# Seven block products for three column groups instead of two, and weight sums added by DMA

## The chip, the cores and the metric

The kernel runs on one core of a Trainium2 chip. Time is device time in microseconds (us) of one execution, the median of several runs. Lower is better.

## The reference, cut to what matters

A decoder trunk of four layers on 256 tokens of width 1024. In each layer a token mixer and a memory attention share one input and one output projection, and a SwiGLU feed-forward follows:

```python
SEQ, D_MODEL, D_FF = 256, 1024, 2816

def _swiglu(x, w_in, w_out):              # w_in: 1024 x 5632, w_out: 2816 x 1024
    gu = x @ w_in
    return (jax.nn.silu(gu[..., :D_FF]) * gu[..., D_FF:]) @ w_out

# for each of the four layers
x = x + jnp.concatenate([mix, mo], axis=-1) @ w_o[i]
x = x + _swiglu(_rmsnorm(x, g_ffn[i]), w_ffn_in[i], w_ffn_out[i])
```

All is float32. The change touches the first feed-forward product (`x @ w_in`) and the part of the second that is computed by the same helper.

## The kernel before, in words

**How a product is made.** Every float32 operand is split into a high and a low part (`wparts`, L128 to L133): ScalarE (ACT) casts the raw weight tile to `whi` (L131), VectorE (DVE) subtracts to get `wlo` (L132). One product of 128 tokens, 128 rows of the weight and 512 columns is then three matmuls (L136 to L138): high by high, high by low, low by high. A weight tile `raw` is 128 partitions by 2 by 512 floats, 512 KB; it is loaded by a DMA that SyncE issues (L124, and L220 in the helper below). The pool of raw tiles has eight buffers, and so have `whi` and `wlo`. A load waits until the tile that had its buffer before has been read for the last time.

**The first feed-forward product** runs over six column groups b = 0 to 5 of w_in: for b = 0 to 4, 512 columns of the gate half and 512 of the up half; for b = 5, 256 of each. A plain group (`proj`, twice) makes 2 token halves x 8 row tiles x 2 sides x 3 = 96 matmuls of 512 columns from 8 raw tiles.

**The helper `strassen`** (L197 to L260) computes the same group as a 2 by 2 block product by seven block products instead of eight: 7 x 12 = 84 matmuls. Its left blocks are sums of token blocks (`ab`), its right blocks are sums of weight blocks. Of the weight blocks b11, b12, b22, b21 (two raw tiles each, s = 0, 1) eight tile sums are needed: t = b11 + b12, b12 += b22, t += b22, t += b21, for each s. In the kernel before all eight are VectorE additions of 128x1024 floats (`plus`, L224). Each right block is then split by `wparts`, so the helper splits 14 tiles, against 8 of a plain group. The tile t (`wsum`) lives in the same pool of eight raw buffers. The matmuls of the helper are L214 to L216; its partial results go through `v`, `u`, `y` (VectorE, 128x512) and the callback `out`.

It is used for b = 1 and b = 4, and once per layer in the second feed-forward product (`hidden_products`, on eight of its 22 row blocks): three times per layer, 12 times in all. For the last use, `hidden_side` builds the token sums from the transposed hidden blocks of b = 3 and b = 4.

**What sets the order.** The engines run side by side, each through its own list, and wait for each other on semaphores. The lists come from a scheduler that reorders within the program's dependences: loads on SyncE's queue, casts on ACT, subtractions and sums on DVE. Small callbacks (`later`, `flush`) put transposes and evacuations between the matmuls. GpSimd (POOL) has little to do: it computes the norms' reciprocal roots (`rstd`, L329 and L330) and a few masks.

Of the kernel before, what the change touches and what calls it, by code (L numbers as in the profile page):

```python
# [13 lines left out]
ALU = mybir.AluOpType  # L14
# [3 lines left out]
P = 128  # L18
# [22 lines left out]
def trunk_kernel(ctx, tc, x, mem, vecs, w_in, w_kv, w_o, w_f1, w_f2, lams, g_final, out):  # L41
    nc = tc.nc
# [85 lines left out]
    def wparts(raw, nk=2, ncol=512):  # L128
        hi = wsplit.tile([P, nk, ncol], F32R, name="whi", tag="whi")
        lo = wsplit.tile([P, nk, ncol], F32R, name="wlo", tag="wlo")  # L130
        nc.scalar.copy(hi, raw)  # L131
        wlast[:] = [nc.vector.tensor_tensor(lo, raw, hi.bitcast(F32), ALU.subtract)]  # L132
        return hi, lo  # L133
# [9 lines left out]
    def later(rounds, f):  # L143
        pend.append([rounds, f])

    def flush():
        for item in pend:
            item[0] -= 1
        for item in [i for i in pend if i[0] <= 0]:
            pend.remove(item)  # L150
            item[1]()
# [45 lines left out]
    def strassen(left, right, ab, out):  # L197

        acc = {}
        banks = {1: 1, 2: 1, 5: 5, 3: 5, 7: 7, 4: 7, 6: 6}

        def product(p, w, s):
            b = banks[p]
            if b not in acc:
                acc[b] = ps_acc.tile([P, 512], F32, name="acc", tag="ps")
            lh, ll = ab[p]  # L210
            for k in range(2):
                kc = 2 * s + k
                start, stop = kc == 0 and p == b, kc == 3
                nc.tensor.matmul(acc[b], lh[:, kc, :], w[0][:, k, :], start=start, stop=False, skip_group_check=True)  # L214
                nc.tensor.matmul(acc[b], lh[:, kc, :], w[1][:, k, :], start=False, stop=False, skip_group_check=True)  # L215
                nc.tensor.matmul(acc[b], ll[:, kc, :], w[0][:, k, :], start=False, stop=stop, skip_group_check=True)  # L216

        def load(cols, r):
            raw = wraw.tile([P, 2, 512], F32, name="raw", tag="raw")
            nc.sync.dma_start(raw, cols[r:r + 2 * P, :].rearrange("(c p) n -> p c n", p=P))  # L220
            return raw

        def plus(out, a, b):
            nc.vector.tensor_tensor(out, a, b, ALU.add)  # L224

        part = lambda name: work.tile([P, 512], F32, name=name, tag="att", bufs=NATT)
        b22, sums = [], []
        v, u, y = part("sv"), part("su"), part("sy")
        for s in range(2):
            b11, b12 = (load(c, 2 * s * P) for c in (left, right))  # L230
            b22.append(load(right, 512 + 2 * s * P))
            product(1, wparts(b11), s)
            t = wraw.tile([P, 2, 512], F32, name="wsum", tag="raw")
            plus(t, b11, b12)
            if s == 1:
                nc.scalar.copy(v, acc[1])
            product(5, wparts(t), s)
            flush()
            plus(b12, b12, b22[s])
            product(7, wparts(b12), s)  # L240
            plus(t, t, b22[s])
            product(6, wparts(t), s)
            flush()
            sums.append(t)
        plus(u, acc[6], v)
        plus(y, acc[7], u)
        b21 = [load(left, 512 + 2 * s * P) for s in range(2)]
        for s in range(2):
            product(2, wparts(b21[s]), s)
        out(0, 0, acc[1], None)  # L250
        out(1, 1, acc[5], y)
        flush()
        for s in range(2):
            plus(sums[s], sums[s], b21[s])
            product(4, wparts(sums[s]), s)
            if s == 1:
                out(1, 0, acc[7], u)
            product(3, wparts(b22[s]), s)
            flush()
        out(0, 1, acc[5], u)  # L260

    def negative(rs):
        out = []
# [443 lines left out]
    for i in range(DEPTH):  # L707
# [136 lines left out]
        hab, hsum = {}, {}  # L844

        def hidden_side(k, t, src):

            tt, stt = nc.vector.tensor_tensor, nc.vector.scalar_tensor_tensor
            if k == 0 and t == 0:
                both = big.tile([P, 2, 4, P], F32, name="hsum", tag="big")  # L850
                hsum["d"], hsum["a21"] = both[:, 0], both[:, 1]
                nc.scalar.copy(hsum["d"], src)
            elif k == 0:
                nc.scalar.copy(hsum["a21"], src)
                tt(hsum["d"], hsum["d"], src, ALU.subtract)
                hab[7] = token_parts(hsum["d"])
            elif t == 1:
                tt(hsum["a21"], src, hsum["a21"], ALU.subtract)
                hab[5] = token_parts(hsum["a21"])
                stt(hsum["d"], hsum["d"], -1.0, src, ALU.mult, ALU.subtract)  # L860
                hab[6] = token_parts(hsum["d"])
            else:
                stt(hsum["a21"], src, -1.0, hsum["d"], ALU.mult, ALU.subtract)
                hab[3] = token_parts(hsum["a21"])
                for p, g, t in ((1, 3, 0), (2, 4, 0), (4, 4, 1)):
                    hab[p] = tuple(x[:, :, t * P:(t + 1) * P] for x in hts[g])

        for b in range(6):
            n = 512 if b < 5 else 256
            if n == 512:  # L870
                hh = big.tile([P, 4, S], F32R, name="hh", tag="big")
                hl = big.tile([P, 4, S], F32R, name="hl", tag="big")
            else:
                both = big.tile([P, 2, 2, S], F32R, name="hb", tag="big")
                hh, hl = both[:, 0], both[:, 1]
            hts.append((hh, hl))
            sg = [work.tile([P, 512], F32, name="sg", tag="qkn", bufs=4) for _ in range(NT)]

            def h_out(t, g_ps, u_ps, hh=hh, hl=hl, sg=sg, n=n, b=b):
                s = sg[t][:, :n]  # L880
                if g_ps is not None:
                    nc.scalar.activation(s, g_ps, AF.Silu, scale=rx[t])
                if u_ps is not None:
                    nc.vector.scalar_tensor_tensor(s, u_ps, rx[t], s, ALU.mult, ALU.mult)
                    later(1, lambda: hidden(t, s, hh, hl, n, b))

            def hidden(t, s, hh, hl, n, b):
                tr = ps_x.tile([P, 4, P], F32, name="tr", tag="ps")
                for c in range(n // P):
                    nc.tensor.transpose(tr[:, c, :], s[:, c * P:(c + 1) * P], ident)  # L890
                src = tr[:, :n // P, :]
                hi = hh[:, :, t * P:(t + 1) * P]
                nc.scalar.copy(hi, src)
                nc.vector.tensor_tensor(hl[:, :, t * P:(t + 1) * P], src, hi.bitcast(F32), ALU.subtract)
                if b in (3, 4):
                    hidden_side(b - 3, t, src)

            c0 = b * 512
            gcols, ucols = w_f1[i, :, c0:c0 + n], w_f1[i, :, DFF + c0:DFF + c0 + n]
            if b in (1, 4):  # L900
                def gated(t, side, ps, add, sg=sg, hh=hh, hl=hl, b=b, up={}):
                    if side == 0:
                        src = ps
                        if add is not None:
                            nc.vector.tensor_tensor(sg[t], ps, add, ALU.add)
                            src = sg[t]
                        nc.scalar.activation(sg[t], src, AF.Silu, scale=rx[t])
                        up[t, 0] = sg[t]
                    else:
                        up[t, 1] = add if t == 1 else work.tile([P, 512], F32, name="sx", tag="att", bufs=NATT)  # L910
                        nc.vector.tensor_tensor(up[t, 1], ps, add, ALU.add)  # L911
                    if (t, 0) in up and (t, 1) in up:
                        nc.vector.scalar_tensor_tensor(sg[t], up[t, 1], rneg[t], sg[t], ALU.mult, ALU.mult)
                        later(2, lambda: hidden(t, sg[t], hh, hl, 512, b))

                strassen(gcols, ucols, ab, gated)
            elif n == 512:
                proj([gcols], xT, lambda t, ps: h_out(t, ps, None))
                if b == 0:
                    ab, rneg = tokens_side(xg, xT), negative(rx)  # L920
                proj([ucols], xT, lambda t, ps: h_out(t, None, ps))
            else:
                proj([gcols, ucols], xT, lambda t, ps: h_out(t, ps[:, :n], ps[:, n:2 * n]))
# [52 lines left out]
```

## Time and profile before

| | |
|---|---|
| median of 3 runs | 1271.62 us (1271.61 to 1271.62) |
| profiled execution, its own time | 1271.41 us |
| span of its instructions | 1269.7 us, so 1.7 us lie around it |
| PE (matmul) busy | 1258.3 us, 99% |
| DVE busy | 1022.4 us, 81% |
| ACT busy | 753.3 us, 59% |
| POOL busy | 55.7 us, 4% |
| DMA engines, mean busy share | 55.6% for 226.31 MB of loads and stores |
| granted TensorE clock | 0.999 |

The page divides the span into 40 slices and gives for each the busy tenths of every engine and of the 16 DMA engines. The matmul rows overlap each other (a matmul is shown for 0.39 us, the next starts before it has ended), so that a rate is read from the starts and not from the durations.

### The profile page before, as it was taken

The numbers are of one execution on the slowest core, as the hardware profiler recorded it, in microseconds if no ns is written. First come the engines' busy times: TensorE is split into PE (matmuls) and PEld (weight loads), VectorE is DVE, ScalarE is ACT, GpSimd is POOL, SyncE is SP. The second block draws the span as 40 slices with busy tenths as digits, with TensorE's granted clock in tenths as the row PEclk, the third lists the DMA queues.
The fourth block names the chain that finished last, engine by engine and source line by source line (L and its number), as shares of the span: only waits on it lengthen the run. The fifth ranks groups of instructions, "written<-read, shape, count | busy, mean of one in ns | idle before, by whom it ended". The sixth has DMA issues, their size and how long they took to land.

```text
span 1269.7 us, 16380 instructions
## 1 busy us (share of the span) xinstructions
PE 1258.3 (99%) x6031; PEld 1036.9 (82%) x6031; DVE 1022.4 (81%) x1271; ACT 753.3 (59%) x1067; POOL 55.7 (4%) x109
## 2 busy tenths in 40 slices
PE   8999999999999999999999999999999999999997
PEld 6888888888888888888888888888888888888886
DVE  6765699899867669989986777989996646997995
ACT  7756466575555646656655545656556655674743
POOL 1000000000111000000000000000000001000001
PEclk9999999999999999999999999999999999999999
DMA  9644538366764444836575563665486444384561
GB/s 345 203 150 133 149 116 276 106 207 193 261 193 130 136 149 116 282 116 219 192 247 172 164 197 103 185 215 180 166 272 209 133 133 149 100 260 138 199 200 66
DMA packets 111888, 227.35 MB, mean 179 GB/s; under 512 B 7488, under 2 KB 20288, under 8 KB 111808
## 3 DMA queue, kind: packets, MB, share of 16 engines
q1 hardware_dynamic: 111808, 226.31, 55.6%
q8 instruction: 47, 0.77, 0.2%
q14 instruction: 33, 0.27, 0.1%
HBM read 225.23 MB, written 1.05 MB: 178 GB/s over the span
## 4 chain that ended last, share of the span: by engine, by line
PE 95%; DVE 2%; ACT 1%; issue 1%; DMA 0%; SPq 0%; POOL 0%; POOLq 0%; ACTq 0%
PE acc L136 23%; PE acc L138 23%; PE acc L137 23%; PE acc L214 6%; PE acc L216 6%; PE acc L215 6%; PE tr L890 2%; PE tr L363 1%; DVE wlo L132 1%; PE tr L349 1%; PE tr L432 1%; PE at L413 1%; PE at L445 1%; PE at L479 1%; PE at L521 1%; DVE wsum L224 1%
## 5 line engine op out<-in xcount | busy, mean ns | idle before, releaser
L132 DVE TENSOR_TENSOR wlo<-raw,whi 128x1024 fp32r<-128x1024 f32 (+1 forms) x428 | 508.0, 1210 | 101.3 <-ACT whi L131 99.0
L131 ACT CAST whi<-raw 128x1024 fp32r<-128x1024 f32 (+1 forms) x428 | 434.1, 1041 | 198.8 <-PE acc L138 122.6
L136 PE MATMUL acc<-whi,xth 128*128 128x512 f32 (+1 forms) x896 | 353.6, 395 | 1.1 <-ACT xth L356 1.1
L137 PE MATMUL acc<-wlo,xth 128*128 128x512 f32 (+1 forms) x896 | 342.9, 383 | 1.3 <-DVE wlo L132 1.3
L138 PE MATMUL acc<-whi,xtl 128*128 128x512 f32 (+1 forms) x896 | 343.9, 384 | 0.0
L138 PEld LDWEIGHTS acc<-whi,xtl 128*128 128x128 f32 x896 | 168.4, 188 | 33.8
L137 PEld LDWEIGHTS acc<-wlo,xth 128*128 128x128 f32 x896 | 168.9, 189 | 32.3 <-DVE wlo L132 2.5
L136 PEld LDWEIGHTS acc<-whi,xth 128*128 128x128 f32 x896 | 168.7, 188 | 32.5 <-ACT xth L356 1.6
L131 ACT CAST whi<-wsum 128x1024 fp32r<-128x1024 f32 x72 | 75.7, 1052 | 85.4 <-DVE wsum L224 81.5
L132 DVE TENSOR_TENSOR wlo<-wsum,whi 128x1024 fp32r<-128x1024 f32 x72 | 87.7, 1218 | 1.5 <-ACT whi L131 0.7
L214 PE MATMUL acc<-whi,sh 128*128 128x512 f32 x192 | 75.9, 396 | 0.0
L136 PE MATMUL acc<-whi,hh 128*128 128x512 f32 x192 | 75.6, 394 | 0.0
L216 PE MATMUL acc<-whi,sl 128*128 128x512 f32 x192 | 74.9, 390 | 0.0
L138 PE MATMUL acc<-whi,hl 128*128 128x512 f32 x192 | 74.8, 390 | 0.0
L215 PE MATMUL acc<-wlo,sh 128*128 128x512 f32 x192 | 74.8, 390 | 0.0
L137 PE MATMUL acc<-wlo,hh 128*128 128x512 f32 x192 | 74.8, 390 | 0.0
L224 DVE TENSOR_TENSOR wsum<-wsum,raw 128x1024 f32<-128x1024 f32 x48 | 57.8, 1218 | 0.3
L136 PE MATMUL acc<-whi,oh 128*128 128x512 f32 x128 | 51.1, 400 | 0.0
L138 PE MATMUL acc<-whi,ol 128*128 128x512 f32 x128 | 50.0, 391 | 0.0
L137 PE MATMUL acc<-wlo,oh 128*128 128x512 f32 x128 | 49.9, 390 | 0.0
L214 PEld LDWEIGHTS acc<-whi,sh 128*128 128x128 f32 x192 | 36.1, 188 | 8.2 <-DVE sy L911 1.1
L216 PEld LDWEIGHTS acc<-whi,sl 128*128 128x128 f32 x192 | 36.1, 188 | 7.7
(236 smaller groups left out, 1762.9 us busy)
## 6 DMA issues: line engine op xcount, KB each, us to landing
raw<-in_w_ffn_in SPq DMA_DIRECT2D x160, 512.0 KB, 4.5
raw<-in_w_in SPq DMA_DIRECT2D x100, 512.0 KB, 4.8
raw<-in_w_ffn_out SPq DMA_DIRECT2D x88, 512.0 KB, 4.4
raw<-in_w_o SPq DMA_DIRECT2D x40, 512.0 KB, 4.1
raw<-in_w_mem_kv SPq DMA_DIRECT2D x16, 512.0 KB, 4.4
raw<-in_w_ffn_in SPq DMA_DIRECT2D x32, 256.0 KB, 3.2
raw<-in_w_in SPq DMA_DIRECT2D x8, 256.0 KB, 5.6
x<-in_x SPq DMA_DIRECT2D x4, 256.0 KB, 3.9
```

Of the source, the lines that this page charges most:

```text
L131: nc.scalar.copy(hi, raw)
L132: wlast[:] = [nc.vector.tensor_tensor(lo, raw, hi.bitcast(F32), ALU.subtract)]
L136: nc.tensor.matmul(ps, lh, wh, start=first, stop=False)
L137: nc.tensor.matmul(ps, lh, wl, start=False, stop=False)
L138: return nc.tensor.matmul(ps, ll, wh, start=False, stop=last)
L214: nc.tensor.matmul(acc[b], lh[:, kc, :], w[0][:, k, :], start=start, stop=False, skip_group_check=True)
L215: nc.tensor.matmul(acc[b], lh[:, kc, :], w[1][:, k, :], start=False, stop=False, skip_group_check=True)
L216: nc.tensor.matmul(acc[b], ll[:, kc, :], w[0][:, k, :], start=False, stop=stop, skip_group_check=True)
L224: nc.vector.tensor_tensor(out, a, b, ALU.add)
L349: last_pe = nc.tensor.transpose(ps[:, c, :], src[:, kc * P:(kc + 1) * P], ident).ins
L363: nc.tensor.transpose(ps[:, c, :], src[:, c * P:(c + 1) * P], ident)
L890: nc.tensor.transpose(tr[:, c, :], s[:, c * P:(c + 1) * P], ident)
```

## The change

Three things are changed.

1. The helper is used for b = 2 as well: four uses per layer instead of three, two of them next to each other (b = 1, b = 2).
2. Of the eight tile sums of a use, two (t = b11 + b12) stay on VectorE. The other six are DMAs that GpSimd issues, from a raw tile in SBUF into another one with `accum_op=add` (`add_by_dma`, L227 and L228 of the changed kernel).
3. The order of the products within the helper is different, so are the places of the two loads of b21: products 1, 5, 1, 5, then 7, 7, the loads of b21, then 6, 6, 2, 2, 3, 3, 4, 4 (before: 1, 5, 7, 6 for each s, 2, 2, then 4, 3, 4, 3). The results come out with (0, 1) before (1, 0), and `hidden_side` follows that: it keeps the transposed block of token half 0 in PSUM until that of half 1 has come.

```diff
+        def add_by_dma(out, a):
+            nc.gpsimd.dma_start(out, a, accum_op=ALU.add)
+
+        b12, b22, sums = [], [], []
         v, u, y = part("sv"), part("su"), part("sy")
         for s in range(2):
-            b11, b12 = (load(c, 2 * s * P) for c in (left, right))
+            b11 = load(left, 2 * s * P)
+            b12.append(load(right, 2 * s * P))
             b22.append(load(right, 512 + 2 * s * P))
             product(1, wparts(b11), s)
             t = wraw.tile([P, 2, 512], F32, name="wsum", tag="raw")
-            plus(t, b11, b12)
+            plus(t, b11, b12[s])
+            add_by_dma(b12[s], b22[s])
             if s == 1:
                 nc.scalar.copy(v, acc[1])
             product(5, wparts(t), s)
-            flush()
-            plus(b12, b12, b22[s])
-            product(7, wparts(b12), s)
-            plus(t, t, b22[s])
-            product(6, wparts(t), s)
+            add_by_dma(t, b22[s])
             flush()
             sums.append(t)
+        for s in range(2):
+            product(7, wparts(b12[s]), s)
+        b21 = [load(left, 512 + 2 * s * P) for s in range(2)]
+        flush()
+        for s in range(2):
+            product(6, wparts(sums[s]), s)
+            add_by_dma(sums[s], b21[s])
         plus(u, acc[6], v)
         plus(y, acc[7], u)
-        b21 = [load(left, 512 + 2 * s * P) for s in range(2)]
         for s in range(2):
             product(2, wparts(b21[s]), s)
         out(0, 0, acc[1], None)
         out(1, 1, acc[5], y)
         flush()
         for s in range(2):
-            plus(sums[s], sums[s], b21[s])
+            product(3, wparts(b22[s]), s)
+        out(0, 1, acc[5], u)
+        flush()
+        for s in range(2):
             product(4, wparts(sums[s]), s)
-            if s == 1:
-                out(1, 0, acc[7], u)
-            product(3, wparts(b22[s]), s)
-            flush()
-        out(0, 1, acc[5], u)
+        out(1, 0, acc[7], u)
...
-            elif t == 1:
+            elif t == 0:
+                hsum["a12"] = src
+            else:
...
-            else:
-                stt(hsum["a21"], src, -1.0, hsum["d"], ALU.mult, ALU.subtract)
+                stt(hsum["a21"], hsum["a12"], -1.0, hsum["d"], ALU.mult, ALU.subtract)
...
-            if b in (1, 4):
+            if b in (1, 2, 4):
```

How the lists of the engines move, at two places. First VectorE's list in the second feed-forward product of the second layer, where the helper's use begins. The numbers name single tiles: before, raw_5619, 5621 and 5623 are b11, b12 and b22 of s = 0, and wsum_5636 is its t.

```order
L132 TENSOR_TENSOR wlo_5626<-raw_5619,whi_5625 128x1024
L224 TENSOR_TENSOR wsum_5636<-raw_5619,raw_5621 128x1024
L224 TENSOR_TENSOR raw_5621<-raw_5621,raw_5623 128x1024
L132 TENSOR_TENSOR wlo_5639<-wsum_5636,whi_5638 128x1024
L132 TENSOR_TENSOR wlo_5651<-raw_5621,whi_5650 128x1024
L224 TENSOR_TENSOR wsum_5636<-wsum_5636,raw_5623 128x1024
L224 TENSOR_TENSOR wsum_5689<-raw_5673,raw_5675 128x1024
L132 TENSOR_TENSOR wlo_5663<-wsum_5636,whi_5662 128x1024
```

The same place in the changed kernel: 5683, 5685 and 5687 are b11, b12 and b22 of s = 0, 5715 and 5717 are b11 and b12 of s = 1, and wsum_5700 and wsum_5731 are the two t.

```order
L132 TENSOR_TENSOR wlo_5704<-wsum_5700,whi_5703 128x1024
L132 TENSOR_TENSOR wlo_5722<-raw_5715,whi_5721 128x1024
L224 TENSOR_TENSOR wsum_5731<-raw_5715,raw_5717 128x1024
L132 TENSOR_TENSOR wlo_5736<-wsum_5731,whi_5735 128x1024
L132 TENSOR_TENSOR wlo_5747<-raw_5685,whi_5746 128x1024
L132 TENSOR_TENSOR wlo_5758<-raw_5717,whi_5757 128x1024
L132 TENSOR_TENSOR wlo_5772<-wsum_5700,whi_5771 128x1024
L132 TENSOR_TENSOR wlo_5784<-wsum_5731,whi_5783 128x1024
```

The in-place sums (`raw<-raw`, `wsum<-wsum,raw`) are gone from VectorE, and splits of tiles that a DMA has added to (raw_5685, raw_5717, then the two wsum) follow each other directly.

Second, GpSimd's list in the feed-forward of the second layer. Before, only the four instructions of the feed-forward norm stand there, and behind them comes the next layer's norm:

```order
L329 TENSOR_SCALAR rstd_4384<-ss_4382 128x1
L330 TENSOR_TENSOR rstd_4384<-rstd_4384,nhalf_99 128x1
L329 TENSOR_SCALAR rstd_4436<-ss_4434 128x1
L330 TENSOR_TENSOR rstd_4436<-rstd_4436,nhalf_99 128x1
L329 TENSOR_SCALAR rstd_5935<-ss_5933 128x1
```

In the changed kernel 24 DMAs stand there as well. These are the norm, the six DMAs of b = 1 and the first two of b = 2 (for each use b12 += b22 and t += b22 for s = 0 and 1, then twice t += b21; in b = 1 raw_4676 and raw_4715 are b12, raw_4678 and raw_4717 b22, raw_4765 and raw_4767 b21):

```order
L228 DMA raw_4676<-raw_4678 128x1024
L335 TENSOR_SCALAR rstd_4416<-ss_4414 128x1
L336 TENSOR_TENSOR rstd_4416<-rstd_4416,nhalf_99 128x1
L335 TENSOR_SCALAR rstd_4468<-ss_4466 128x1
L336 TENSOR_TENSOR rstd_4468<-rstd_4468,nhalf_99 128x1
L228 DMA raw_4715<-raw_4717 128x1024
L228 DMA wsum_4691<-raw_4678 128x1024
L228 DMA wsum_4729<-raw_4717 128x1024
L228 DMA wsum_4691<-raw_4765 128x1024
L228 DMA wsum_4729<-raw_4767 128x1024
L228 DMA raw_4871<-raw_4873 128x1024
L228 DMA wsum_4886<-raw_4873 128x1024
```

One DMA stands ahead of the feed-forward norm, 23 behind it. Each of them waits on GpSimd's queue for its two tiles, and those behind it wait with it.

More of the change, by code (lines that the diff above doesn't have):

```diff
@@ L226, in strassen @@
         part = lambda name: work.tile([P, 512], F32, name=name, tag="att", bufs=NATT)
-        b22, sums = [], []
+        def add_by_dma(out, a):
+            nc.gpsimd.dma_start(out, a, accum_op=ALU.add)
+        b12, b22, sums = [], [], []
         v, u, y = part("sv"), part("su"), part("sy")
         for s in range(2):
-            b11, b12 = (load(c, 2 * s * P) for c in (left, right))
+            b11 = load(left, 2 * s * P)
+            b12.append(load(right, 2 * s * P))
             b22.append(load(right, 512 + 2 * s * P))
```

## The prediction

> **What bounds the kernel now.** I first read the page's head and the stalls of TensorE.
>
> ```profile
> span 1269.7 us, 16380 instructions
> PE 1258.3 (99%) x6031; PEld 1036.9 (82%) x6031; DVE 1022.4 (81%) x1271; ACT 753.3 (59%) x1067; POOL 55.7 (4%) x109
> PE 95%; DVE 2%; ACT 1%; issue 1%; DMA 0%; SPq 0%; POOL 0%; POOLq 0%; ACTq 0%
> PE acc L137 <- DVE wlo L132: 1.3, 3, 0.8
> ```
>
> TensorE is the path: 95% of the chain, and the longest of its waits for another engine is 1.3 us in total. So matmuls that go away are time that goes away, as long as the other engines keep up. What a matmul is worth has to be read from starts, since the rows overlap. Two rows of a plain group, with 36 matmuls from the first to the second:
>
> ```profile
> 170.08 0.39 PE L136 MATMUL acc<-whi,xth 128*128 128x512 f32 x1
> 178.24 0.39 PE L136 MATMUL acc<-whi,xth 128*128 128x512 f32 x1
> ```
>
> That is (178.24 - 170.08) / 36 = 0.2267 us, not the 0.39 us of a row. A plain group of 96 takes 21.8 us of TensorE, a group by seven products (84) takes 19.0 us.
>
> The view by stages shows who else is near the limit. The second line is the group b = 1 by seven products, the third the plain b = 2, the last one a whole feed-forward of the second layer:
>
> ```profile
> core 0: us, PE busy (x) PEld busy (x) DVE busy (x) ACT busy (x) POOL busy (x), PEclk, DMA share, GB/s
> 184.20:204.00 19.80, 19.80 (x90) 16.01 (x89) 19.77 (x22) 13.57 (x16) 0.00 (x0) 1.00 0.62 193
> 204.00:226.00 22.00, 22.00 (x104) 18.07 (x103) 18.60 (x19) 12.78 (x16) 0.00 (x0) 1.00 0.81 277
> 470.00:646.00 176.00, 176.00 (x803) 144.81 (x802) 164.21 (x179) 109.05 (x130) 1.49 (x4) 1.00 0.58 185
> ```
>
> In a group by seven products VectorE has no gap at all (19.77 of 19.80 us), and in the whole feed-forward it works 93%. The DMA engines work 58% there. So TensorE is first and VectorE is just behind it; the change takes work from both and gives work to the DMA engines.
>
> How far the splits run ahead of TensorE decides what a late split costs. VectorE's first split for b = 1 and TensorE's first matmul of it:
>
> ```profile
> 173.77 1.22 DVE L132 TENSOR_TENSOR wlo<-raw,whi 128x1024 fp32r<-128x1024 f32 x1
> 184.17 0.39 PE L214 MATMUL acc<-whi,xth 128*128 128x512 f32 x1
> ```
>
> The lead is 184.17 - 173.77 = 10.4 us, and more it cannot be: eight split buffers of six matmuls last 8 x 6 x 0.2267 = 10.9 us.
>
> **The change part by part.**
>
> *The third group, on TensorE.* 12 matmuls fewer per layer, 48 in all: 48 x 0.2267 = -10.9 us. All of it is on the path. This is the whole gain there can be.
>
> *VectorE and ACT.* These rows carry it:
>
> ```profile
> L224 DVE TENSOR_TENSOR wsum<-wsum,raw x48: 1208/1218/1227, 177.8 to 1232.7; 128x1024 f32<-128x1024 f32 x48
> L224 DVE TENSOR_TENSOR wsum<-raw x24: 1217/1223/1483, 151.7 to 1217.2; 128x1024 f32<-128x1024 f32 x24
> L224 DVE TENSOR_TENSOR raw<-raw x24: 1210/1224/1227, 153.4 to 1221.9; 128x1024 f32<-128x1024 f32 x24
> 307.06 1.22 DVE L132 TENSOR_TENSOR wlo<-wsum,whi 128x1024 fp32r<-128x1024 f32 x1
> 308.19 0.68 DVE L936 TENSOR_TENSOR x<-x,acc 128x512 f32<-128x512 f32 x1
> ```
>
> 96 sums become 32. One takes 1.22 us in its row, but the next instruction starts 1.13 us after it (308.19 - 307.06). VectorE loses 64 x 1.13 = 72 us, and gains 6 more splits in each of the four new uses, 24 x 1.13 = 27 us, beside their partial results (`u`, `y` and the callbacks). ACT gains 24 casts of 1.05 us at 59% load. None of it is on the path, so I cost it at nothing; TensorE's 99% covers it. In one use VectorE has 14 splits and two sums left, 16 x 1.13 = 18.1 us beside its partial results, against 22 x 1.13 = 24.9 us before. The `tr` block that is now kept in PSUM holds one of eight banks a little longer; I cost it at nothing for the same reason.
>
> *The accumulating DMAs.* There are 6 x 16 = 96. The trace shows none. Two prices matter, the time each takes of the 16 DMA engines, S, and the time until it has landed. For S the nearest rows are those of the loads:
>
> ```profile
> PE   8999999999999999999999999999999999999997
> DMA  9644538366764444836575563665486444384561
> GB/s 345 203 150 133 149 116 276 106 207 193 261 193 130 136 149 116 282 116 219 192 247 172 164 197 103 185 215 180 166 272 209 133 133 149 100 260 138 199 200 66
> L220 SPq DMA_DIRECT2D raw<-in_w_ffn_in x64: 367/368/689, 142.1 to 1164.4; - x64
> DMA to landing us min/median/max: 3.5/4.0/6.4
> ```
>
> In the first slice the engines are full at 345 GB/s, so that a 512 KB load takes 524,288 / 345,000 = 1.52 us of them. An accumulating DMA writes as many bytes as a load, so I put the lower bound at S = 1.52. It reads two operands, its source and its destination; if the two reads simply add, S = 3.04. I take the middle, 2.28: two streams are read, but from SBUF and not from HBM. For the landing, a load needs at best 3.5 us, 1.98 more than its 1.52; with SyncE's 0.37 us to issue, an accumulating DMA lands 0.37 + 2.28 + 1.98 = 4.6 us after its turn, and 2.28 later, 6.9 us, where a load shares the engines with it. I take the mean, 5.8 us. The VectorE sum that it replaces took 1.13 us, so each tile comes 4.6 us later.
>
> The Trainium skill prices such a DMA too. In "Collectives: The Full Stack", section "The bandwidth ceiling: the fold count and why AG ≠ RS ≠ AR", it says of an adding DMA that it "isn't slower because the CCE add costs cycles — it's slower because the add needs two source reads", at half the rate. No row here shows it. By it S is 3.04, which is the second rival below.
>
> Now the DMA engines' sum for one use of the helper: eight loads, 8 x 1.52 = 12.2 us, and six accumulating DMAs, 6 x 2.28 = 13.7 us, together 25.8 us, while TensorE wants the group in 19.0 us. They fall behind by 6.8 us per use. Over the whole feed-forward they do not: 0.58 x 176 = 102 us now, with 24 x 2.28 = 55 us more 157 of 173 us. So what counts is the lead at the start of a use. It is 10.4 us behind a plain group, and the later landing takes 4.6 of it, which leaves 5.8 us. Two uses in a row (b = 1, b = 2) fall behind by 13.6 us, 7.8 more than that; the single ones (b = 4 and the second product) by 6.8, 1.0 more. That is 7.8 + 1.0 + 1.0 = 9.8 us of waiting per layer, 39 us in four layers.
>
> What stands behind such a wait: on POOL the next DMAs of the use, in order, and at one place the norm's `rstd`, whose result VectorE waits for already.
>
> ```profile
> DVE rneg L266 <- POOL rstd L330: 8.0, 8, 1.5
> SPq L124 <- DVE wlo L132: 653.5, 274, 12.5
> SPq L220 <- DVE wlo L132: 279.7, 87, 15.3
> ```
>
> On SyncE's queue the loads stand behind a buffer that is not free: 87 loads of the helper already wait 279.7 us for a split to be done. A tile that is split later is freed later, and the next group's loads with it. On VectorE the splits that follow each other in the list wait for the one whose tile has not landed.
>
> *The sum.* 1271.4 (the profiled execution's own time) - 10.9 + 39 = 1299.5 us. The runs' median is 0.2 us above that execution, so I say 1300.
>
> **The rivals.**
>
> *First: the DMAs are hidden, the kernel is faster.* With S = 1.52 a use needs 12.2 + 9.1 = 21.3 us, falls behind by 2.2, two in a row by 4.5; the landing is then 0.37 + 1.52 + 1.98 to 1.52 more, on the mean 4.6 us, 3.5 later than the sum. The lead left is 6.9 us, more than 4.5. Then nothing waits and the time is 1271.6 - 10.9 = 1260.7 us; the last us may go to VectorE, which still has some 24 us per use with its partial results. For it: the DMA engines have 42% of the feed-forward free, and SBUF reads may overlap each other. Against it: two operands through an engine at the price of one.
>
> *Second: the two reads add, much slower.* S = 3.04: a use needs 30.4 us, 11.4 too many. The landing is 5.4 to 8.4, on the mean 6.9 us, 5.8 later, which leaves 4.6 us of lead. Per layer (22.8 - 4.6) + 2 x (11.4 - 4.6) = 31.8 us of waiting, 127 in all: 1271.6 - 10.9 + 127 = 1388 us. For it: the plain count of bytes read. Against it: the reads are not from HBM, which may be what limits a load.
>
> *Third: no change.* Waiting and gain are equal where the two uses in a row lose 2.7 us per layer. With lead 10.4 - (0.37 + 1.5 S + 1.98 - 1.13) = 9.2 - 1.5 S and a lag of 2 x (12.2 + 6 S - 19.0), that is at S = 1.90. This is also the point from which the change decides against itself: above 1.90 us of DMA time per sum it is slower, below it is faster. A narrow case, some 0.05 us of S on either side.
>
> A price of issue enters too: SyncE's 0.37 us is a hardware queue's row, POOL's is not shown. In "DMA: Bandwidth & Descriptors", section "Specifications", the Trainium skill gives a first byte after about 1 us for DMAs from GpSimd and 0.6 for those of SyncE; by an estimate from that, each landing is 0.4 us later, and the sum 0.4 x 3 x 4 = 5 us higher. No row here shows it.
>
> **How the numbers follow.** A difference of 0.2% is about what a measurement of this kernel can tell from none. I give my forecast (S between about 1.95 and 2.7) a chance of 0.47; the hidden DMAs 0.25; the added reads, or anything slower than S = 2.7, 0.20; no change 0.08. So faster 0.25, same 0.08, slower 0.67. The likeliest case's own range is 1275 to 1350. The range reaches down to the first rival's 1260.7 and a little below, and up to 1380, which takes in the cheaper part of the second: 1259 to 1380.
>
> **What would show each step right or wrong.** TensorE should have 48 matmuls fewer, and its starts still be 0.2267 us apart where it runs. In the list of DMA issues the accumulating ones should land some 5 to 7 us after their issue; at 4 us the first rival is right, at 8 and more the second. In the table by stages the DMA share of the two groups in a row should be over 0.9, and the waits of TensorE should name `wlo` or `whi` of the helper's splits, those of ACT the accumulating DMAs. VectorE should show gaps in these groups where it now has none. My forecast is wrong if TensorE's idle time stays near its present 11 us, and my reason is wrong if the idle time is there while the DMA engines are not full: then it is the landing or the queue on POOL, and not the engines' time.

## The result and the profile after

The changed kernel takes 1328.52 us (median of 4 runs, 1327.49 to 1330.04), the kernel before 1271.61 us: a ratio of 1.0448 with a 95% interval of 1.0433 to 1.0464. It is 56.9 us slower. The forecast was slower by 28 us, with the time measured inside its range: the direction was right, the size was half of what came.

The head of the page, the row of the granted clock in 40 slices (in tenths of full speed) and the row of GpSimd's DMA queue (packets, MB, share of 16 engines), after the change:

```profile
span 1327.4 us, 16744 instructions
PE 1270.3 (96%) x5983; PEld 1039.7 (78%) x5983; DVE 989.3 (75%) x1251; ACT 778.9 (59%) x1095; POOL 139.0 (10%) x205
PEclk9999999999999999899999999998999999989999
...
q0 software_dynamic: 13824, 50.34, 20.4%
```

The clock's row of the kernel before, for comparison:

```profile
PEclk9999999999999999999999999999999999999999
```

The first two rows split the loss. The span grew by 1327.4 - 1269.7 = 57.7 us. TensorE's idle time was 1269.7 - 1258.3 = 11.4 us and is now 1327.4 - 1270.3 = 57.1 us: 45.7 us more. But its busy time grew too, by 12.0 us, although 48 matmuls (6031 - 5983), worth 10.9 us, are gone. So TensorE's busy time for the matmuls that are left is 22.9 us longer than it was. The clock's row shows where most of it lies: in some slices the granted clock has an 8, in the profile before it has none. The three terms are -10.9 + 45.7 + 22.9 = 57.7 us; the last is what is left over, so they add up by construction.

TensorE's waits, the longest first (in total, times, longest):

```profile
PE tr L897 <- DVE sg L920: 16.4, 4, 4.4
PE tr L897 <- DVE sg L891: 13.7, 4, 3.9
```

These eight waits, two per layer, make up 30.1 us of the idle time. They name neither a split nor a DMA but a transpose (L897) that waits for an evacuation `sg` by VectorE (VectorE's last step on a product before it is transposed). What holds the evacuation is seen in time. These rows are from the timeline around the first of the eight, in the group b = 2 (start, duration, then the idle time before and what ended it):

```profile
204.71 0.87 POOL L228 DMA_DIRECT2D raw<-raw  x1 [1.99 <-DVE wsum L224]
...
212.56 1.04 ACT L131 CAST whi<-raw 128x1024 fp32r<-128x1024 f32 x1 [6.17 <-DMA raw<-raw]
213.64 1.23 DVE L132 TENSOR_TENSOR wlo<-raw,whi 128x1024 fp32r<-128x1024 f32 x1 [4.16 <-ACT whi L131]
...
214.78 0.75 DVE L920 SCALAR_TENSOR_TENSOR sg<-sy,rneg,sg 128x512 f32<-128x512 f32 x1
...
215.68 1.00 PE L897 MATMUL tr<-ident,sg 128*128 128x128 f32 x4 [4.07 <-DVE sg L920]
```

TensorE's own rows after it:

```profile
216.90 0.63 PE L215 MATMUL acc<-wlo,sh 128*128 128x512 f32 x1
217.33 0.63 PE L216 MATMUL acc<-whi,sl 128*128 128x512 f32 x1
217.75 0.63 PE L214 MATMUL acc<-whi,sh 128*128 128x512 f32 x1
```

GpSimd issues the second accumulating DMA of the use at 204.71. Its tile can be cast at 212.56, 7.85 us later. ACT stands 6.17 us in front of that cast, VectorE 4.16 us in front of the subtraction behind it. The evacuation `sg` (L920) stands behind that subtraction in VectorE's list, and the transposes wait for the evacuation. After the wait matmuls start 0.43 us apart (216.90, 217.33, 217.75) and not 0.2267. The DMA of 204.71 was issued 0.4 us after the sum on VectorE that it waits for had ended (203.09 + 1.21 = 204.30), so GpSimd's queue did not hold it back here; by the trace it landed at 212.49, 7.8 us after its issue.

The table by stages around the same place, and one microsecond of the second layer's wait, which ends at 545.90 (columns as in the prediction's table; the last three are granted clock, DMA share and GB/s):

```profile
215.00:216.00 1.00, 0.32 (x2) 0.35 (x3) 1.00 (x2) 1.00 (x2) 0.00 (x0) 0.90 0.42 115
216.00:217.00 1.00, 1.00 (x6) 0.90 (x5) 1.00 (x2) 1.00 (x3) 0.00 (x0) 0.50 0.70 125
...
544.00:545.00 1.00, 0.00 (x0) 0.00 (x0) 1.00 (x1) 1.00 (x3) 0.00 (x0) 0.50 0.85 301
```

Around each of the eight waits, which last 3.05 to 4.36 us, the granted clock is 0.50, for 3.4 us in five cases and for 6.8 us in three; a ninth such stretch, of 3.4 us, stands at a wait of 2.25 us. In four of the nine the clock is down well before the wait ends (third row), and that part costs nothing. Where matmuls run at this clock, 3.4 us of it cost about 1.7 us beside the wait. In stretches of 10 us, twelve have a clock below 0.995 before the last 10 us of the span; the first of them:

```profile
210.00:220.00 10.00, 5.93 (x21) 4.62 (x21) 6.36 (x7) 7.43 (x10) 1.74 (x2) 0.83 0.81 199
```

(1 - clock) x 10 us, summed over the twelve, is 20.5 us, in pieces of about 1.7 or 3.4; the kernel before has no such stretch outside its last 20 us. Of these, 17.7 us lie in time in which TensorE works, by the trace; that is most of the 22.9. The rest fits the ends of rows: TensorE stops for more than 0.2 us 30 times in place of 7, and at each stop the last matmul counts with its 0.39 us and not with 0.2267, an estimate of 23 x 0.16 = 4 us.

The Trainium skill ("TensorE: Matmul & The Clock Gate", section "HAM oscillation — how this bites in real kernels") says that TensorE should have no idle gaps above about 3.4 us, since the clock then falls to half. The trace agrees that the clock falls to half (0.50), but not in the limit: here waits of 3.05 and 3.15 us have a slow stretch too, and so has one of 2.25 us. In the first experiment below no wait is above 2.1 us, and the clock fell all the same, at several short ones.

### The profile page after: what moved, and what is told of

Read it like the earlier page. It is cut to its first block, busy times and chain, and to the rows that moved or that the text cites. A ratio compares the mean times of both kernels' runs of the same rounds, so it can differ in the third digit from the quotient of the medians.

```text
span 1327.4 us, 16744 instructions
## 1 busy us (share of the span) xinstructions
PE 1270.3 (96%) x5983; PEld 1039.7 (78%) x5983; DVE 989.3 (75%) x1251; ACT 778.9 (59%) x1095; POOL 139.0 (10%) x205
## 5 line engine op out<-in xcount | busy, mean ns | idle before, releaser
L136 PE MATMUL acc<-whi,xth 128*128 128x512 f32 (+1 forms) x768 | 303.8, 396 | 10.5 <-ACT whi L131 9.6
L137 PE MATMUL acc<-wlo,xth 128*128 128x512 f32 (+1 forms) x768 | 293.1, 382 | 1.9 <-DVE wlo L132 1.9
L138 PE MATMUL acc<-whi,xtl 128*128 128x512 f32 (+1 forms) x768 | 293.9, 383 | 0.0
L132 DVE TENSOR_TENSOR wlo<-wsum,whi 128x1024 fp32r<-128x1024 f32 x96 | 116.6, 1219 | 28.6 <-ACT whi L131 28.1
L215 PE MATMUL acc<-wlo,sh 128*128 128x512 f32 x256 | 102.8, 402 | 0.0
L228 POOL DMA_DIRECT2D wsum<-raw x64 | 55.4, 865 | 251.7 <-DVE wlo L132 155.4
L228 POOL DMA_DIRECT2D raw<-raw x32 | 28.3, 884 | 440.2 <-DVE wsum L224 119.3
L215 PE MATMUL acc<-wlo,xth 128*128 128x512 f32 x144 | 59.1, 411 | 2.1 <-DVE wlo L132 2.1
L214 PE MATMUL acc<-whi,xth 128*128 128x512 f32 x144 | 60.7, 421 | 0.4
L897 PE MATMUL tr<-ident,sg 128*128 128x128 f32 x176 | 30.4, 296 | 30.2 <-DVE sg L920 16.4
```

What stands on the lines that cost most here:

```text
L136: nc.tensor.matmul(ps, lh, wh, start=first, stop=False)
L137: nc.tensor.matmul(ps, lh, wl, start=False, stop=False)
L138: return nc.tensor.matmul(ps, ll, wh, start=False, stop=last)
L228: nc.gpsimd.dma_start(out, a, accum_op=ALU.add)
```

## The experiments

Three questions are put: whether the accumulating DMAs cause the loss or the third group itself; whether it is their engine time, their number or where they stand; and what the clock has to do with it. Each kernel ran beside the kernel before on the same chip (1271.73 to 1271.79 us), to which its ratio is taken.

### Sums on VectorE, three groups

```diff
         def add_by_dma(out, a):
-            nc.gpsimd.dma_start(out, a, accum_op=ALU.add)
+            plus(out, out, a)
```

> The changed kernel with all eight tile sums on VectorE again; three groups and the new order of products stay. Theory L (the late landing of the accumulating DMAs is the cost): no accumulating DMA is left to wait for, TensorE idles about 11 us as in the kernel before, the clock is back at 0.999, and the 48 matmuls are gained: 1261 to 1266 us. Rival Q (two uses of the helper next to each other are more than the splits can follow, whoever makes the sums): VectorE then needs 22 x 1.13 + some 5.6 = 30.5 us per use against 19.0 of TensorE, two in a row fall behind by 23 us, 12.6 more than the lead of 10.4, 50 us in four layers: 1305 to 1330 us, with waits for wlo and for the partial results in b = 2.

1323.22 us, ratio 1.0402 [1.0387, 1.0418]. Taking the accumulating DMAs out brings back only 5 us. The table by stages, the stretch of the group b = 2:

```profile
204.00:224.00 20.00, 14.56 (x62) 10.20 (x60) 20.00 (x22) 14.13 (x17) 0.00 (x0) 1.00 0.36 105
```

VectorE works 20.00 of 20.00 us, TensorE 14.56. Here VectorE is the bound: with eight sums per use it needs longer than TensorE's 19.0 us, and behind b = 1 there is no plain group any more in which it catches up. The clock falls here too (0.988 over the span), and around short waits. TensorE's rows with a wait in the same group of the second layer, and one microsecond of the table behind them:

```profile
536.43 0.50 PE L215 MATMUL acc<-wlo,sh 128*128 128x512 f32 x1 [0.48 <-DVE wlo L132]
539.96 0.50 PE L215 MATMUL acc<-wlo,xth 128*128 128x512 f32 x1 [1.67 <-DVE wlo L132]
542.23 0.79 PE L214 MATMUL acc<-whi,sh 128*128 128x512 f32 x1 [0.84 <-ACT whi L131]
```

```profile
545.00:546.00 1.00, 1.00 (x4) 0.71 (x4) 1.00 (x2) 0.50 (x1) 0.00 (x0) 0.50 0.00 0
```

So the loss cannot be put down to the DMAs alone. Each of the ways of making these sums that was tried, by DMA, on VectorE and (below) on GpSimd, is too slow for two uses in a row.

### The old order and VectorE sums, three groups

```diff
-            if b in (1, 4):
+            if b in (1, 2, 4):
```

(in the kernel before)

> The kernel before with one thing changed: the helper for b = 2 as well. All eight sums on VectorE, the old order of products. Theory Q (two uses next to each other outrun the splits, whatever makes the sums; after the run with all sums on VectorE and the new order took 1323.2 us): the order matters little, 1305 to 1330 us. Rival (the new order of the products is what costs in that run): 1262 to 1285 us.

1320.92 us, ratio 1.0385 [1.0367, 1.0402], within 2.3 us of the run above. The order of the products is not what makes three groups slow. The granted clock is 0.996 here and 0.988 there (a loss of some 5 and 15 us), and the times are nearly equal all the same: a lower clock does not go one to one into the time.

### Two groups, with the accumulating DMAs

```diff
-            if b in (1, 2, 4):
+            if b in (1, 4):
```

> The changed kernel with the helper for b = 1 and b = 4 only; the six accumulating DMAs per use and the new order stay. Theory L: the second tile of b12 lands as late in each use, so the waits at b = 4 and in the second product stay (3.9 + 1.7 + 1.3 us per layer after), with their share of the lower clock: 1290 to 1310 us. Rival Q: uses with a plain group ahead of them have the lead to cover the landing: 1265 to 1275 us.

1285.29 us, ratio 1.0106 [1.0091, 1.0121]; 43 us less than with three groups. In the profiled execution the granted clock is 0.999 (0.995 in the three others, which take 2 to 5 us more), and TensorE's longest wait is 2.2 us:

```profile
PE acc L214 <- DVE sy L224: 8.8, 8, 2.2
```

The row of the accumulating DMAs' queue on its page:

```profile
q0 software_dynamic: 10368, 37.75, 16.2%
```

The span here is 1281.0 us, so one accumulating DMA takes 0.162 x 1281.0 / 72 = 2.88 us of the 16 engines; in the changed kernel, by its row above, it is 0.204 x 1327.4 / 96 = 2.82.

### Two groups, sums on VectorE, new order

```diff
-            add_by_dma(b12[s], b22[s])
+            plus(b12[s], b12[s], b22[s])
...
-            if b in (1, 2, 4):
+            if b in (1, 4):
```

(and so for the other two sums)

> The changed kernel with b = 1 and b = 4 only and all eight sums on VectorE: of the change only the new order of the products is left. If the order costs nothing, this is the kernel before again, 1269 to 1274 us, and the 13.6 us of the run with two groups and DMA sums (1285.3) belong to the DMAs. If the order is what costs there, it is near 1285 us.

1274.29 us (10 runs), ratio 1.0020 [1.0010, 1.0029]. This is the kernel before with the new order of the products alone: it costs 2.5 us. Against the run with two groups and DMAs, the DMAs cost 1285.3 - 1274.3 = 11.0 us even where plain products follow each use.

### Plain copies in place of accumulating DMAs

```diff
-            nc.gpsimd.dma_start(out, a, accum_op=ALU.add)
+            nc.gpsimd.dma_start(out, a)
```

This kernel leaves out six of the eight sums of a use.

> The changed kernel with each accumulating DMA replaced by a plain copying DMA from GpSimd between the same two tiles, with the same waits. Six of the eight sums are left out. If reading the second operand is what makes them dear, the time of the DMA engines for one falls from 2.8 to about 1.5 us, the landing from 6.1 to under 5 us, and the kernel takes 1275 to 1300 us. If the descriptors that GpSimd writes or the queue behind the loads set the landing, it stays near 6 us, and the kernel near 1325 us.

1285.14 us (2 runs), ratio 1.0105 [1.0085, 1.0126]. The same number of DMAs between the same tiles, in the same places and with three groups, is 43 us faster when they copy. The span is 1284.4 us. The queue's row on the page, then the answer for the issuing line (issue on GpSimd in ns, landing in us), then the longest of TensorE's waits:

```profile
q0 software_dynamic: 13824, 50.34, 9.8%
```

```profile
L228 POOL DMA_DIRECT2D wsum<-raw x64: 527/527/539, 176.8 to 1239.4; - x64
DMA to landing us min/median/max: 2.9/4.0/6.7
```

```profile
PE tr L897 <- DVE sg L920: 8.1, 4, 3.0
```

And the issuing line of the changed kernel:

```profile
L228 POOL DMA_DIRECT2D wsum<-raw x64: 850/862/885, 177.1 to 1284.6; - x64
DMA to landing us min/median/max: 4.5/6.1/9.7
```

A copy takes 0.098 x 1284.4 / 96 = 1.31 us of the engines, an accumulating DMA 2.82, a ratio of 2.15. A copy lands at 4.0 us in place of 6.1 in the median, and GpSimd spends 0.53 us on its issue in place of 0.86. The Trainium skill's two source reads ("Collectives: The Full Stack", "The bandwidth ceiling: the fold count and why AG ≠ RS ≠ AR"), the rule that the prediction cited, stand there for the reduction between cores and mean half the rate of a copy; 2.15 is near that. The longest wait in front of the transposes falls from 4.4 to 3.0 us, and the clock of the profiled execution is 0.999 (0.997 in the other run). Which of the three prices does it (engine time, landing, issue) this run cannot say, since all three move together. Two numbers speak for the engines' time without proving it: the quickest landings differ by 4.5 - 2.9 = 1.6 us, nearly the 1.51 us by which the engine times differ, and in the stretch 184 to 204 us the engines are busy 0.84 of the time with copies (this row), where with accumulating DMAs they are full (1.01 in 180 to 200 us, a row further below):

```profile
184.00:204.00 20.00, 20.00 (x92) 16.41 (x91) 18.59 (x20) 13.46 (x16) 2.65 (x5) 1.00 0.84 286
```

### No sums at all

```diff
-            nc.gpsimd.dma_start(out, a, accum_op=ALU.add)
+            pass
```

> The changed kernel without the six sums: neither a DMA nor VectorE makes them, the products use the tiles as they are (the output lacks these sums). If the supply of the sums is all that stands between the change and its 10.9 us, this takes 1260 to 1263 us with the clock at 0.999. If three groups also ask too much of the loads, of ACT or of the 14 splits per use, it stays at 1268 us or more.

1263.38 us, ratio 0.9934 [0.9919, 0.9948]. This kernel leaves the six sums out. With the sums for nothing, 8.4 of the 10.9 us that the removed matmuls are worth arrive; the other 2.5 are as much as the new order of the products costs in the run with two groups and VectorE sums. So the gain is there, and the price of the six sums is 1328.5 - 1263.4 = 65.1 us.

### Two groups next to each other

```diff
-            if b in (1, 2, 4):
+            if b in (1, 2):
```

> The run with two groups and DMA sums (1285.3 us) with the helper at b = 1 and b = 2 in place of b = 1 and b = 4: as many uses, matmuls, loads and accumulating DMAs, but next to each other. Theory Q (two uses in a row are what cannot be followed): the pair's waits of the changed kernel come back (0.7 + 4.1 + 1.2 us per layer) with their slower matmuls: 1300 to 1315 us. If it does not matter that they are neighbours: 1282 to 1289 us.

1304.33 us, ratio 1.0256 [1.0240, 1.0271]. The counts are those of the run with b = 1 and b = 4; only the place differs, and that costs 19 us. The wait is the one seen above:

```profile
PE tr L897 <- DVE sg L920: 18.4, 4, 4.7
```

The clock is 0.989 here, and between 0.988 and 0.993 in all four executions.

### The half group between them

```diff
-        for b in range(6):
+        for b in (0, 1, 5, 2, 3, 4):
```

(and `hts` as a dictionary, so that each hidden block keeps its number)

> The changed kernel with its six accumulating DMAs per use, but the column groups in the order 0, 1, 5, 2, 3, 4: the half group b = 5 stands between the two uses that were next to each other. Nothing else is changed. Theory Q: what counts is that two uses follow each other; apart, each costs what it cost with two groups (1285.3 - 1271.7 = 13.6 us for 12 uses, 1.1 each), so 1271.7 - 10.9 + 16 x 1.1 = 1279 us, up to 1290 since the half group restores only part of the lead. Theory L (each use waits for its own landings): little changes, 1310 to 1330 us.

1322.5 us, ratio 1.0394 [1.0378, 1.0409]: 6 us better than the change, no more. The long waits in front of transposes now name the evacuation of groups without the helper (`sg` L891: 19.0 us, 7 times), and there is a new one:

```profile
PE acc L214 <- ACT whi L131: 8.7, 3, 5.0
```

The edit does more than it was meant for: the half group no longer stands between b = 4 and the second product, and there, at 330 us, is the new wait of 4.96 us. So it is no clean test of the distance; the run before this one is.

### The late split held back

```diff
-            product(7, wparts(b12[s]), s)
+            with ExitStack() as held:
+                if s == 1 and start_evacs:
+                    held.enter_context(tc.issue_after(start_evacs[0].ins))
+                parts = wparts(b12[s])
+            product(7, parts, s)
```

(`start_evacs` is the last evacuation of the group before.) If the evacuation is late only because it stands behind a late split in VectorE's list, then putting the split behind it should remove the eight waits. The edit holds the split's cast on ACT back as well.

> The changed kernel with one constraint on the order more: the split of the second b12 tile of a use is issued after the last evacuation of the group before (VectorE's product sg), so that no evacuation stands behind the tile that lands last. Theory P (it is the place in VectorE's list that costs: TensorE waits for transposes of sg, not for a split): the 30 us of waits for sg and the slower matmuls behind them go, 1285 to 1305 us. Theory S (the sums come too late for the products as well): the waits move from the transposes to whi and wlo, 1318 us or more.

1376.32 us, ratio 1.0824 [1.0808, 1.0840], 48 us slower than the change; the granted clock is 0.972.

```profile
PE acc L137 <- ACT whi L132: 39.3, 8, 6.9
PE acc L215 <- DVE sy L225: 21.4, 9, 4.9
```

The transposes wait no more, but the matmuls do, and longer (line numbers are one higher here). So the place in the list is where the lateness shows, and the supply of split tiles is late as well. That splits which are held back give up lead for good is the likely reason for the 48 us, but no run separates it.

### Filling TensorE's wait

To test the clock by itself, matmuls on the identity were put in front of the two transposes that wait longest, 36 of them in a first kernel, 16 in a second:

```diff
+                if b in (1, 3) and t == 1:
+                    for k in range(36):
+                        nc.tensor.matmul(tr[:, k % 4, :], ident, ident, start=True, stop=True, skip_group_check=True)
```

> The changed kernel with 36 matmuls of 128 columns of the identity (about 4 us) ahead of the two transposes per layer that wait about 4 us each; they need nothing that is late and their result is written over. If the lower clock (0.984) is a consequence of TensorE standing still for 4 us, the clock is 0.995 or more and the time falls by most of the 23 us that the matmuls lost, to 1305 to 1315 us, although TensorE does more. If the clock is low for another reason, it stays near 0.984 and the time is 1326 us or more.

> As the run with filling matmuls, but 16 of them at each of the eight places: each runs in two passes of 0.111 us, so these take 3.6 us, about what TensorE waits there, and not 8.0. Clock theory: the granted clock is 0.995 or more, the matmuls are as short as in the kernel before, and the time falls under that of the changed kernel by 8 to 22 us: 1306 to 1320 us. If the lower clock costs nothing that shows in the time, or if the fill itself delays what follows, 1325 us or more.

The first took 1376.4 us, 1.0835 [1.0814, 1.0856]; each matmul of the fill shows as two, 72 in all and 8.2 us per place, twice the wait that it should fill. The second took 1358.53 us, 1.0680 [1.0665, 1.0696]. Neither came out as expected: both are slower than the change, and the granted clock over the span, forecast at 0.995 or more, is 0.993 and 0.980 (0.984 in the changed kernel). The second's timeline at the first place, and the granted clock there:

```profile
212.23 3.73 PE L898 MATMUL tr<-ident 128*128 128x128 f32 x32
217.12 0.65 PE L900 MATMUL tr<-ident,sg 128*128 128x128 f32 x4 [1.15 <-DVE sg L923]
228.93 0.79 PE L136 MATMUL acc<-whi,xth 128*128 128x512 f32 x1 [2.97 <-ACT whi L131]
```

```profile
210.00:220.00 10.00, 8.85 (x58) 7.81 (x57) 5.09 (x7) 5.90 (x8) 0.80 (x1) 1.00 0.82 199
228.00:234.00 6.00, 3.81 (x8) 2.72 (x9) 6.00 (x7) 4.30 (x5) 0.00 (x0) 0.56 1.04 388
```

Where TensorE was kept busy the clock stayed at 1.00 (in the changed kernel it is 0.83 in the same 10 us). But the next wait came some 12 us later, with a clock of 0.56 around it, and the total rose. Locally this speaks for the idle time as the cause of the slower clock, at one place; over the whole kernel it is not shown. What the clock costs in total the two runs don't tell, since the fill is itself work on the engine that sets the end.

### The sums on GpSimd

```diff
-            nc.gpsimd.dma_start(out, a, accum_op=ALU.add)
+            nc.gpsimd.tensor_tensor(out, out, a, ALU.add)
```

> The changed kernel with the six sums as additions on GpSimd's compute engine in place of the accumulating DMAs. By the row of 128x512 additions there (1.28 us) one takes about 2.5 us, six 15 us per use against 19.0 of TensorE, with no landing. If GpSimd and VectorE do not disturb each other: 1262 to 1275 us, below the kernel before if all of the 10.9 us comes through. The Trainium skill says in SBUF — State Buffer, section Summary: rules for kernel authors, that a VectorE instruction with two SBUF inputs and a GpSimd instruction that reads SBUF block each other; by that, the splits get as much longer as the additions take, and the time is 1320 us or more.

1406.65 us, ratio 1.1055 [1.1036, 1.1073], the slowest. Two groups of the tile `wsum` (min, median and max in ns), GpSimd's sum and VectorE's subtraction behind it:

```profile
L228 POOL TENSOR_TENSOR wsum<-wsum,raw x64: 2359/3303/4412, 182.0 to 1360.9; 128x1024 f32<-128x1024 f32 x64
L132 DVE TENSOR_TENSOR wlo<-wsum,whi x96: 1206/1214/3198, 175.1 to 1369.3; 128x1024 fp32r<-128x1024 f32 x96
```

GpSimd's sum takes 2.4 to 4.4 us, and VectorE's subtraction up to 3.2, against 1.23 at most in the changed kernel:

```profile
L132 DVE TENSOR_TENSOR wlo<-wsum,whi x96: 1210/1218/1228, 175.3 to 1290.8; 128x1024 fp32r<-128x1024 f32 x96
```

Of these 96 subtractions, the 52 that overlap no sum on GpSimd take 1.22 us at most, the 44 that overlap one 2.39 in the median. So GpSimd's sum holds VectorE up. That VectorE holds GpSimd up too fits the spread of 2.4 to 4.4 us, but there is no run of these sums with VectorE idle beside them.

## Why the prediction was right and wrong

*The gain.* Right. 48 matmuls are gone, worth 10.9 us, and with free sums 8.4 of them arrive. The new order of the products, to which the prediction gives no cost, is as much as the rest: 2.5 us in the run that has it alone.

*VectorE and ACT at nothing.* Right for the path: VectorE works 75% of the span with the DMAs, 81% before. What the prediction left out is the other side of it: with VectorE sums in three groups the kernel would have been as slow (1321 to 1323 us). It looked for the danger in the DMAs and didn't ask whether the kernel before could have borne a third group at all. Its own row would have told: VectorE had no gap in a use, and 22 x 1.13 = 24.9 us of it beside the partial results stand against TensorE's 19.0.

*An accumulating DMA's price.* Mis-sized. S was taken as 2.28 between 1.52 and 3.04; it is 2.82, near the added reads and outside the forecast's own 1.95 to 2.7, in the case that was given 0.20 ("the added reads, or anything slower than S = 2.7"). The landing was forecast at 5.8 us from its turn and is 6.1 from its issue, in the middle, 9.7 at most. The issue was priced at SyncE's 0.37 us; GpSimd takes 0.86.

*The sum of waiting.* 39 us were forecast, 45.7 came; but the two agree by errors that cancel. With the measured S and landing the same formula gives a use 12.2 + 16.9 = 29.1 us, 10.1 too many, and a lead left of 10.4 - (6.1 - 1.13) = 5.4, so per layer (20.2 - 5.4) + 2 x (10.1 - 5.4) = 24.2, in all 97 us. So the formula counts too much there. With the copies' numbers it counts too little: S = 1.31 and a landing of 4.0 give a pair's lag of 2 x (12.2 + 7.9 - 19.0) = 2.2 us against a lead of 10.4 - (4.0 - 1.13) = 7.5, so no waiting at all, and that run idles 1284.4 - 1253.0 = 31.4 us, 20.0 more than the kernel before. So the waits do not come about as the formula has it, and its closeness to 45.7 is luck. Its split was wrong as well. TensorE's rows with a wait in the first layer's feed-forward, beside the two long ones:

```profile
199.76 0.49 PE L215 MATMUL acc<-wlo,xth 128*128 128x512 f32 x1 [0.69 <-DVE wlo L132]
...
227.31 0.50 PE L136 MATMUL acc<-whi,xth 128*128 128x512 f32 x1 [1.20 <-ACT whi L131]
...
274.99 0.50 PE L136 MATMUL acc<-whi,xth 128*128 128x512 f32 x1 [1.69 <-ACT whi L131]
...
329.98 0.47 PE L214 MATMUL acc<-whi,hh 128*128 128x512 f32 x1 [1.28 <-DVE sy L224]
```

Here the pair lost 6.0 us (0.69 + 4.07 + 1.20, forecast 7.8) and the second product 1.3 (forecast 1.0), but the single use b = 4 lost 5.6 (3.87 + 1.69) where 1.0 was forecast. A single late tile was enough for that. These rows of the timeline are from b = 4:

```profile
250.59 0.86 POOL L228 DMA_DIRECT2D raw<-raw  x1 [1.41 <-DVE wsum L224]
...
259.82 1.04 ACT L131 CAST whi<-raw 128x1024 fp32r<-128x1024 f32 x1 [5.69 <-DMA raw<-raw]
260.89 1.23 DVE L132 TENSOR_TENSOR wlo<-raw,whi 128x1024 fp32r<-128x1024 f32 x1 [6.04 <-ACT whi L131]
...
262.04 0.75 DVE L891 SCALAR_TENSOR_TENSOR sg<-acc,rstd,sg 128x512 f32<-128x512 f32 x1
...
262.84 0.65 PE L897 MATMUL tr<-ident,sg 128*128 128x128 f32 x4 [3.87 <-DVE sg L891]
```

The tile of the DMA issued at 250.59 could be cast 9.2 us later. The formula works with a mean landing, while the lists, in which each instruction waits for the one ahead of it, pass on the latest one.

*The step that failed* is "1271.4 - 10.9 + 39 = 1299.5": a term is missing from it. The sum lets TensorE run at 0.2267 us per matmul as soon as its wait is over ("its starts still be 0.2267 us apart where it runs"). It does not: around the long waits the granted clock is 0.50 and the starts are 0.43 us apart, for 3.4 or 6.8 us, and TensorE's busy time grows by 22.9 us, some 18 of it by the clock. With this term the sum is 1299.5 + 22.9 = 1322; the 6.7 us of idle time that the waiting was short (45.7 - 39) lead to 1329.1, the time of the profiled execution.

*The signs.* The landing was in the range named (5 to 7 us) in the median, and the DMA share was as forecast: above 0.9 around b = 1 (first row), while the late DMA of b = 2 was under way, from 204.71 to 212.49 (next two rows), and at b = 4 too:

```profile
180.00:200.00 20.00, 19.31 (x89) 15.61 (x88) 17.43 (x19) 14.74 (x17) 3.23 (x4) 1.00 1.01 270
200.00:210.00 10.00, 9.89 (x45) 7.99 (x45) 8.52 (x10) 2.36 (x3) 2.60 (x3) 1.00 1.02 253
210.00:216.00 6.00, 1.93 (x9) 1.32 (x9) 2.36 (x3) 3.44 (x5) 0.00 (x0) 0.98 0.90 213
248.00:260.00 12.00, 10.97 (x51) 8.76 (x49) 5.99 (x6) 2.88 (x4) 2.59 (x3) 1.00 1.06 234
```

(The share is the time of the packets that start in a stretch, so it can pass 1 a little.) By the prediction's own sign its reason, the engines' time, is borne out at this place: the engines were full until the late tile had landed. In 210 to 220 us as a whole the share is 0.81 (the row of the clock above), but most of that lies behind the landing. The waits were to name `wlo` or `whi` of the helper's splits; most name `sg`, which stands behind such a split. ACT's waits do name the accumulating DMAs. VectorE's gaps are there: it works 17.43 of 20 us around b = 1 (first row above), and its waits for a cast come to 189.7 us, 99.7 in the kernel before:

```profile
ACT whi L131 <- DMA raw<-raw: 68.8, 14, 6.4
```

```profile
DVE wlo L132 <- ACT whi L131: 189.7, 143, 6.0
```

*The rivals.* The hidden DMAs fell with S = 2.82. They would have fallen at S = 1.52 too: the copies, at 1.31, take 1285 us and not 1260.7. So the border at S = 1.90 does not hold either; a faster kernel would have needed sums at a price near zero. The added reads had nearly the right price of a DMA (3.04 against 2.82) and the wrong time (1388), because of the formula.

*What stays open.* Which of engine time, landing and issue makes the difference of 43 us between copies and accumulating DMAs; the full engines speak for the first. What the waits would cost at a constant clock. Whether more raw and split buffers would hide the sums, or whether buffers that come free later hold up the loads; that wasn't tried. No version with all its sums was faster than the kernel before.

## What to carry to other kernels

Work taken from the engine that sets the end is a gain only as far as its suppliers keep up, and this is decided stage by stage: two uses next to each other cost 19 us more than two apart, with equal totals. An accumulating DMA between SBUF tiles is no free adder: here one took the engines' time of two copies and landed 4.5 to 9.7 us after its issue. Look for what stands behind its reader in the lists. Price a long wait of TensorE with the slower matmuls around it: here the lower clock stands for some 18 us of the loss, beside 45.7 us of waiting.

## What was not expected of the hardware

- The granted clock at 0.50 for 3.4 or 6.8 us around waits of 2.25 to 4.36 us; and also, in the kernel with VectorE sums, around waits of 0.5, 1.7 and 0.8 us within 6 us. A wait of 2.96 us in the kernel with copies has none.
- An accumulating DMA of 512 KB takes 2.82 us of the 16 engines against 1.31 for a copy, and 0.86 us of GpSimd's time for its issue against 0.53.
- Beside sums on GpSimd the two-operand instructions of VectorE stretch from 1.22 to as much as 3.2 us; the sums themselves take 2.4 to 4.4 us.
